# Two residual gates reach all partitions through the tensor engine instead of through DMA

## The chip, the cores and the metric

The kernel runs on one core of one Trainium2 chip. The metric is device microseconds (us) of one execution, lower is better.

## The reference

One layer of a hybrid diffusion backbone, for 512 latent tokens and 256 context tokens of 1024 channels, all in float32. What matters here is the modulation of the latent stream and where its six parts go:

```python
sh1, sc1, gt1, sh2, sc2, gt2 = adaln(c, w_ada, b_ada)         # silu(c) @ w_ada + b_ada, 1024 values each
h = modulate(rms_norm(x, g_mix), sh1, sc1)
mix = concat(fourier_mix(u), rec_mixer(q, v, ...)) @ w_out     # u, q, v, two forget gates, g = split(h @ w_in)
x = x + gt1 * mix
x = x + gt2 * ec_moe(modulate(rms_norm(x, g_ffn), sh2, sc2), ...)   # 16 experts, 64 tokens each
return rms_norm(x, g_final)
```

The gates gt1 and gt2 scale the columns of a product whose rows are tokens, so the kernel wants each of them as one row of 1024 values that stands on every partition.

## The kernel before, in words

**The stages.** Up to about 320 us of the profile the mixer runs (modulation, the input projection in segments of 512 columns, the gated recurrence per head, the Fourier groups), then the output projection and the routing, and from about 370 us the sixteen experts, whose weights (554 MB) stream through a ring of 13 slots of SBUF. The ring's first loads (`load_ahead`, line 1354) wait in SP's queue until the memory of the mixer is free.

**The input projection.** A float32 product is made from high and low parts: ACT casts a loaded half tile to its high part (`split`, line 304), POOL or DVE subtracts it for the low part (line 309), and TensorE runs three matmuls per block (`mm3`, lines 145 to 147). A segment has four steps; the weights of the next step are loaded and split while a step runs. A segment's results stand in four PSUM banks for the latent tokens (`acc`) and, where the context is projected too, in two banks (`c`). The banks `m` and `z` exist once each. In the first step of a segment the units go bank after bank, the two context banks last, with 12 matmuls of 256 columns for each. The segments here are `ff` and `fb` (forward and backward forget gates) and then `v`.

**The modulation's second and third group.** `AdaGroup` 1 holds gt1 and sh2, `AdaGroup` 2 holds sc2 and gt2, 2048 columns each. `step` loads 128 rows of `w_ada` (1 MB, tile `adabuf`, three in turn, line 378 in SP's queue) and DVE adds their products to `adaacc` (lines 383, 385). `finish` adds over the partitions on TensorE (line 398, bank `z`), DVE adds the bias into a row tile `adag` (line 400), and four transposes into bank `m` (line 403, `adagT`) put the values in columns. The row tile has tag `gcc` with two buffers:

```python
brow = pc.tile([P, 512], F32, tag="gcc", bufs=2, name=f"brow{g}")    # 390
row = pc.tile([P, 512], F32, tag="gcc", bufs=2, name=f"adag{g}")     # 395
g = pc.tile([P, 2, CT], F32, tag="gcc", bufs=2, name=f"gcc{d}_{b}")  # 543, in ctx_states
```

so the second tile of the context's states (line 543), which POOL opens with a memset (line 544) and DVE fills (lines 549, 551), takes over the buffer of the row and has to wait until all that reads the row has done so. Its transposes (`kcT`, line 558, bank `m`), ACT's copy of them (line 560) and the products `s0p` (line 566) follow.

**The gates.** The row of gt1 is in `adag` of group 1, on partitions 0 and 32 (512 values each). Two transfers in ACT's queue (line 589) read each of these rows 128 times and write the tile `gt1b` (128 x 1024, 512 KB). gt2 is on partitions 64 and 96 of group 2's row; two transfers (line 615) read them 64 times each into `gt2b` (128 x 512, 256 KB: the first half of the channels on partitions 0 to 63, the second on 64 to 127). `gt1b` is read by `gate_cols` (line 915), first at 235 us, `gt2b` by line 1459, first at 442 us.

**What sets the order.** Each engine executes its instructions in one fixed order, written when the program is built. From line 517 to 666, where the change lies, a list scheduler makes that order from the order of the code and from estimated times; from line 667 on, the order on PE, DVE, ACT and POOL is the one of the code. The sigmoids of lines 526 and 532 (ACT) evict a segment's banks; the second of line 526 frees the last context bank for the next segment.

Of the kernel before, what the change touches and what calls it, by code (L numbers as in the profile page):

```python
# [51 lines left out]
# columns of the packed small operands  # L52
# [8 lines left out]
# and of its matrices  # L61
# [4 lines left out]
# columns of the packed shape constants  # L66
# [16 lines left out]
def hybrid_kernel(ctx: ExitStack, tc, x, ctxt, small, const, pos, w_ada, b_ada, w_in, w_out,  # L83
# [13 lines left out]
    # ------------------------------------------------------------------ memory that stays  # L97
# [25 lines left out]
    # ------------------------------------------------------------------ loads, in the order of use  # L123
# [31 lines left out]
    # ------------------------------------------------------------------ adaLN  # L155
    # silu(c) | silu(c_ctx), padded to one column group
    # forget-gate floor: softmax of the logits over the layers, first row
# [18 lines left out]
    class AdaFirst:  # L176
        """Shift and scale of the mixer for channel blocks 2n and 2n+1."""

        def __init__(self, n):
            self.n = n  # L180
            if n % 2 == 0:
                # the memory of the values and of the context's gates
                w = p1b.tile([P, 2, 4, 256], F32, tag="v", name=f"adaw{n}_v")
                self.w = [w[:, 0], w[:, 1]] + [pc.tile([P, 4, 256], F32, tag=f"fctx{d}", name=f"adaw{n}_{d}")
                                               for d in range(2)]
            else:
                self.w = [wst.tile([P, 4, 256], F32, tag="wh" if t % 2 else "wl", bufs=SB, name=f"adaw{n}_{t}")
                          for t in range(4)]
            for t in range(4):
                # half of the rows of both halves of the sum  # L190
                h, a = divmod(t, 2)
                c0 = a * D + n * 256
                for half in range(2):
                    k0 = 4 * half + 2 * h
                    nc.sync.dma_start(self.w[2 * a + half][:, 2 * h:2 * h + 2],
                                      w_ada[k0 * P:(k0 + 2) * P, c0:c0 + 256].rearrange("(b p) d -> p b d", p=P))

        def part(self, t):
            if t == 0:
                self.acc = bank("m" if self.n == 0 else "z", f"adaA{self.n}")  # L200
            # shifts and scales, each from the first and the last half of the sum: partial sums 2a + b // 2
# [7 lines left out]
        def finish(self):  # L209
# [8 lines left out]
            # row r of the pair, shift or scale, channel block  # L218
# [10 lines left out]
    # ------------------------------------------------------------------ normalise and transpose  # L229
    # the transposed rows wait in the memory of the gates  # L230
# [28 lines left out]
    # high and low parts, channel blocks 4-7 and 0-3  # L259
# [23 lines left out]
    # ------------------------------------------------------------------ input projection  # L283
    class Segment:
        """Columns col..col+512 of the projection, four steps of 256 channels each."""
# [10 lines left out]
        def split(self, kk, a, high=None, low=None):  # L296
            """High and low parts of half a tile."""
# [16 lines left out]
        def units(self, kk):  # L314
            """One step, in units of one 128x128 block of weights against all its tokens."""
# [33 lines left out]
            if kk in self.by_bank:  # L349
                # bank after bank: the last finish, and the next's first are needed, one by one  # L350
# [16 lines left out]
    class AdaGroup:  # L367
        """Columns g*2048..(g+1)*2048 of the modulation of the latent stream."""
# [4 lines left out]
        def step(self, k):  # L373
# [6 lines left out]
            # the products per channel of the sum; the tensor engine adds over the partitions  # L380
# [7 lines left out]
        def finish(self):  # L388
# [15 lines left out]
            return row, raw(tp[:], 0, [[32, 4], [P, 4]])  # L404
# [13 lines left out]
    # columns that add the partial sums  # L418
# [3 lines left out]
    # the first segment follows the modulation by quarters of the channels  # L422
    opening = ExitStack()
    opening.enter_context(tc.manual_schedule(engines={EN.PE, EN.DVE, EN.Activation, EN.Pool, EN.SP}))
    # the clock of the tensor engine rises with its activity, so it is kept active until the rows are there
# [35 lines left out]
    for n in range(4):  # L461
        for k in (2 * n, 2 * n + 1):
            if n == 0:
                # the first weights meanwhile
                modulate(k, 0, lambda: sq.split(0, k, nv.tensor_copy, nv if k == 0 else ng))
            else:
                modulate(k, 0)
# [39 lines left out]
    # the gates, per head: forward, backward, queries  # L507
# [31 lines left out]
    def ctx_states(d):  # L539
        """Final states of the context in one direction, two heads at a time."""  # L540
        gs = []
        for b in range(2):
            g = pc.tile([P, 2, CT], F32, tag="gcc", bufs=2, name=f"gcc{d}_{b}")
            ng.memset(g[:, :, CT - 1:CT] if d == 0 else g[:, :, 0:1], 1.0)
            for a in range(2):
                # running product of the later (earlier) gates
# [3 lines left out]
            # minus the decayed keys  # L550
# [33 lines left out]
    arow1, atp = ag1.finish()  # L584
    sh2 = pz.tile([P, NK], F32, name="sh2")
    nv.tensor_copy(sh2.rearrange("p (j i) -> p j i", j=2), atp[:, 2:4, :])
    for j in range(2):
        src = arow1[32 * j:32 * j + 1, :]
        ns.dma_start(gt1b[:, j * 512:(j + 1) * 512],
                     bass.AP(src.tensor, src.offset, [list(src.ap[0]), [0, P], [1, 512]]))  # L590
# [17 lines left out]
    arow2, atp = ag2.finish()  # L608
    a2 = pz.tile([P, NK], F32, name="a2")
    nv.scalar_tensor_tensor(a2.rearrange("p (j i) -> p j i", j=2), atp[:, 0:2, :], 1.0,  # L610
                            sm[:, C_GFFN:C_GFFN + 8].rearrange("p (j i) -> p j i", j=2),
                            op0=ALU.add, op1=ALU.mult)
    for j in range(2):
        src = arow2[64 + 32 * j:65 + 32 * j, :]
        ns.dma_start(gt2b[64 * j:64 * j + 64, :],
                     bass.AP(src.tensor, src.offset, [list(src.ap[0]), [0, 64], [1, 512]]))
# [6 lines left out]
    class Filler:  # L623
        """Work without close dependences, to be issued between the steps of the heads.

        What waits for a unit's matmuls is issued behind the next unit's.
        """
# [17 lines left out]
        def take(self, n):  # L645
            """Issues units; returns the tensor engine's time, negative where nothing should follow at once."""
# [22 lines left out]
    # the table of the function that the gate needs, loaded ahead  # L669
# [27 lines left out]
    # ------------------------------------------------------------------ HGRN2 heads  # L697
# [8 lines left out]
    def head_init(h):  # L706
        f, q = fq[:, h, 0:2, :], fq[:, h, 2, :]
        # slots: keys forward, queries backward, queries forward, keys backward
# [3 lines left out]
        def merge(B, g):  # L712
            # keys: forward in the first half of a pair of blocks, backward in the second
# [31 lines left out]
    def head_scores(h):  # L745
        """Decayed keys and queries by doubling, with the scores of each level."""
# [71 lines left out]
    def lead(n):  # L818
        # units between a step and what it waits for
# [86 lines left out]
    # ------------------------------------------------------------------ output projection, weights  # L906
# [6 lines left out]
    def gate_cols(k, a, eng):  # L913
        # the residual gate scales the columns
# [19 lines left out]
    # ------------------------------------------------------------------ Fourier groups  # L934
# [3 lines left out]
    def after_u():  # L938
        u_sb = p1b.tile([P, NH, S], F32, tag="u", name="u_sb")

        def wo_step(k, n):
            # the weights of the output projection, a piece at a time
# [30 lines left out]
        def fold(g, eng):  # L973
            # positions m and 512-m folded: even part for the cosines, odd part, in place, for the sines
# [18 lines left out]
        def positions(g):  # L993
# [10 lines left out]
            def evict():  # L1004
                # positions 0 and 256 of the cosines; even frequencies stand first
# [93 lines left out]
    class Steps:  # L1099
        """A generator with the tensor engine's time of each step."""  # L1100
# [19 lines left out]
    def fill_to(t, n=99):  # L1120
        """Issues units until the tensor engine has t us of work, n at most."""
# [41 lines left out]
    # ------------------------------------------------------------------ output projection, residual  # L1163
    px = tc.alloc_tile_pool(name="px", bufs=1, side="left", reuse_waits="tile")
    acc_x = px.tile([P, 4, D], F32, name="acc_x")
    # expert weights: one ring of equal slots
# [12 lines left out]
    # ------------------------------------------------------------------ routing  # L1179
# [20 lines left out]
    # rows of shifts through the router, the same on every partition  # L1200
    sh2r = pq.tile([P, NK, P], F32, tag="x2t", bufs=2, name="sh2r")
    ng.tensor_copy(sh2r, sh2[:, :, None].to_broadcast([P, NK, P]))
    # the largest values so far, then those of a token block
    cand = [pq.tile([NE, (CAP if i in (1, 2) else 0) + P], F32, name=f"cand{i}") for i in range(4)]
    # the largest of the first three blocks and of the last, in order
# [5 lines left out]
    # nothing, above the least, equal to it  # L1211
# [45 lines left out]
    def top(n):  # L1257
        """The CAP largest values of a row of candidates, in order."""
# [13 lines left out]
    # the routing of a token block runs between the products of the next ones  # L1272
# [27 lines left out]
    # the largest of two ordered lists: the larger of each value and its opposite in the other  # L1300
# [4 lines left out]
    # chosen are the tokens above the least of the largest, and the first of those equal to it  # L1305
# [5 lines left out]
    # places: those above in order, then the equal ones; places past CAP are no slot's  # L1311
# [22 lines left out]
    # ------------------------------------------------------------------ experts  # L1334
# [27 lines left out]
    # the memory of the first hidden rows holds a slot's worth before  # L1362
# [18 lines left out]
    for e in range(NE):  # L1381
# [26 lines left out]
        # the hidden rows, and their transpose  # L1408
# [7 lines left out]
        # one-hot rows of the slots with their gates, transposed  # L1416
# [13 lines left out]
        # inner index half*1408 + p*11 + r on partition p  # L1430
# [11 lines left out]
        for s8 in range(8):  # L1442
# [4 lines left out]
            # runs of one row half that lie in this slot  # L1447
# [21 lines left out]
    # the last expert goes down in blocks of columns, so that little is left after its last load  # L1469
# [5 lines left out]
    # the final gain on every partition  # L1475
# [12 lines left out]
    def down_last(n):  # L1488
# [3 lines left out]
        for ih in range(2):  # L1492
# [4 lines left out]
            for r in range(NROW):  # L1497
                # two partial sums, of even and odd rows, that the combination adds
# [7 lines left out]
    def combine_last(n, db):  # L1506
# [6 lines left out]
        for b in range(0, 4, nb):  # L1513
# [12 lines left out]
            # final norm  # L1526
# [31 lines left out]
def _shape_constants():  # L1558
# [6 lines left out]
    # the rows of the sines in the order 256, 255 .. 129 and 128, 127 .. 1  # L1565
# [57 lines left out]
```

## Time and profile before

| | |
|---|---|
| runs | 1670.42, 1672.88, 1674.80 us; median 1672.88 |
| span of the profiled execution, first to last instruction | 1668.7 us |
| busy, share of the span | PE 92%, DVE 24%, ACT 15%, POOL 10% |
| DMA, mean over the span | 363 GB/s from HBM, 424 GB/s in most slices after 375 us |

The profile is of one execution of its own; it gives the span, 4.2 us under the median of the runs, and no other time for it. In the rows below, L followed by a number is a line of the code, `x4` counts instructions that are merged in one row, and a bracket holds the idle time of the engine before the instruction and what ended it. PE is TensorE, SPq and ACTq are the queues in which SP and ACT issue transfers (q1 and q10 in the list of DMA queues). PEclk is TensorE's granted clock, 1.00 being 2.4 GHz.

### The profile page before, as it was taken

To read this page: it belongs to the slowest core of one execution; us is meant where nothing else is said; L and a number is where in the kernel's file an instruction comes from. 1 tells how busy PE (TensorE), PEld (TensorE's weight loads), DVE (VectorE), ACT (ScalarE), POOL (GpSimd) and SP (SyncE) were. 2 spreads that over 40 slices of the span, in tenths; PEclk is the share of its full clock that TensorE was granted. 3 is DMA by queue.
4 is the path that set the end of the run, shared out by engine and by line. 5 is a ranking of instruction groups with operands and counts; after the bars stand their busy time and mean duration, and the time that the engine had idled before them with its cause. 6 is when DMAs were issued, how large, how long until landed. Compare 5 with 4: busy or idle time off the path is not lost.

```text
span 1668.7 us, 19918 instructions
## 1 busy us (share of the span) xinstructions
PE 1529.1 (92%) x8519; PEld 753.1 (45%) x8519; DVE 399.8 (24%) x754; ACT 255.9 (15%) x578; POOL 164.8 (10%) x153
## 2 busy tenths in 40 slices
PE   9978998989999999999898989988988899889897
PEld 6766776874443334343433343334333433243335
DVE  4855678370201010201011001100110111011103
ACT  4512456331000001000100010001000100010002
POOL 2623547400000000000000000000000000000002
PEclk9999999999999989999999998999999989999899
DMA  9785211859999999999999999999999999999998
GB/s 346 283 218 136 77 59 58 334 215 357 422 425 423 424 423 423 423 424 423 424 423 424 424 424 424 423 424 424 423 424 423 423 424 423 424 424 423 424 384 257
DMA packets 91448, 608.37 MB, mean 365 GB/s; under 512 B 8152, under 2 KB 30424, under 8 KB 41184
## 3 DMA queue, kind: packets, MB, share of 16 engines
q1 hardware_dynamic: 90480, 605.21, 88.6%
q10 hardware_dynamic: 880, 1.89, 1.5%
q8 instruction: 67, 1.10, 0.3%
q14 instruction: 21, 0.17, 0.0%
HBM read 604.18 MB, written 2.10 MB: 363 GB/s over the span
## 4 chain that ended last, share of the span: by engine, by line
DMA 48%; PE 41%; DVE 5%; ACT 2%; issue 1%; POOL 1%; SPq 0%; POOLq 0%; DVEq 0%; ACTq 0%
DMA uw<-in_wu_dram 18%; DMA gw<-in_wg_dram 15%; DMA dw<-in_wd_dram 12%; PE dn L1455 9%; PE g L1403 7%; PE u L1403 6%; PE gp L1375 4%; PE cb L1464 3%; DMA fb1r<-in_w_in_dram 1%; DMA adabuf<-in_w_ada_dram 1%; ACT xst L1377 1%; DVE X L795 1%; PE op L146 1%; PE op L145 1%; PE op L147 1%
## 5 line engine op out<-in xcount | busy, mean ns | idle before, releaser
L1455 PE MATMUL dn<-dw,hid 128*64 128x512 f32 (+1 forms) x1440 | 315.9, 562 | 9.0 <-DMA dw<-in_wd_dram 9.0
L1403 PE MATMUL u<-uw,xst 128*64 128x512 f32 (+1 forms) x1464 | 298.1, 559 | 23.4 <-DMA uw<-in_wu_dram 23.3
L1403 PE MATMUL g<-gw,xst 128*64 128x512 f32 (+1 forms) x1440 | 300.3, 569 | 0.0
L1403 PEld LDWEIGHTS u<-uw,xst 128*64 128x64 f32 x1464 | 102.7, 137 | 216.0 <-issue 165.1
L1455 PEld LDWEIGHTS dn<-dw,hid 128*64 128x64 f32 x1440 | 113.9, 136 | 168.1 <-issue 126.5
L1403 PEld LDWEIGHTS g<-gw,xst 128*64 128x64 f32 x1440 | 102.7, 139 | 187.0 <-issue 181.6
L1429 DVE TENSOR_TENSOR hid<-u,hid 128x512 f32<-128x512 f32 (+1 forms) x48 | 30.3, 647 | 538.5 <-PE u L1403 522.6
L1464 PE MATMUL cb<-ye,oht 64*128 64x512 f32 x240 | 108.9, 742 | 26.6 <-DVE acc_x L1467 15.6
L1415 ACT ACTIVATE hid<-g 128x512 f32<-128x512 f32 (+1 forms) x48 | 26.7, 561 | 655.2 <-PE g L1403 654.5
L1473 POOL COPY gt2f<-gt2b 64x512 f32<-64x512 f32 x2 | 1.2, 606 | 1265.8 <-DVE hid L1429 1265.8
L1375 PE MATMUL gp<-oh,xn 128*128 128x128 f32 x512 | 84.0, 294 | 23.3 <-ACT xst L1377 23.1
L1375 PEld LDWEIGHTS gp<-oh,xn 128*128 128x128 f32 x512 | 65.0, 190 | 74.5 <-issue 40.0
L1467 DVE TENSOR_TENSOR acc_x<-cb,acc_x 128x512 f32<-128x512 f32 x120 | 78.6, 688 | 57.6 <-PE cb L1464 57.6
L1377 ACT ACTIVATE xst<-gp,sh,a 128x128 f32<-128x128 f32 x64 | 29.3, 457 | 335.2 <-PE gp L1375 178.9
L1464 PEld LDWEIGHTS cb<-ye,oht 64*128 64x128 f32 x240 | 35.3, 206 | 97.2 <-DVE acc_x L1467 73.0
L1459 DVE TENSOR_TENSOR ye<-dn,gt2b 128x512 f32<-128x512 f32 x15 | 10.4, 692 | 214.9 <-PE dn L1455 214.9
L1437 ACT COPY hid<-hT 128x512 f32<-128x512 f32 (+1 forms) x48 | 24.8, 549 | 170.2 <-PE hT L1435 170.2
L1385 DVE TENSOR_TENSOR oh<-iota,posm 128x512 f32<-128x512 f32 x8 | 5.5, 692 | 182.8 <-PE gp L1375 182.7
L385 DVE SCALAR_TENSOR_TENSOR adaacc<-adabuf,cs,adaacc 128x1024 f32<-128x1024 f32 x28 | 44.3, 1642 | 5.1 <-DMA adabuf<-in_w_ada_dram 5.1
L1419 DVE TENSOR_SCALAR ohg<-iota,posm,aff 128x128 f32<-128x128 f32 x64 | 17.9, 343 | 103.2 <-PE ohT L1424 103.2
L1435 PE MATMUL hT<-ident,hid 128*128 128x128 f32 x176 | 29.3, 300 | 7.7 <-DVE hid L1429 5.9
L1435 PEld LDWEIGHTS hT<-ident,hid 128*128 128x128 f32 x176 | 23.9, 212 | 16.0 <-DVE hid L1429 11.6
(602 smaller groups left out, 1530.6 us busy)
## 6 DMA issues: line engine op xcount, KB each, us to landing
uw<-in_wu_dram SPq DMA_DIRECT2D x122, 1408.0 KB, 27.1
dw<-in_wd_dram SPq DMA_DIRECT2D x120, 1408.0 KB, 27.1
gw<-in_wg_dram SPq DMA_DIRECT2D x120, 1408.0 KB, 27.1
adabuf<-in_w_ada_dram SPq DMA_DIRECT2D x16, 1024.0 KB, 6.4
gw0a<-in_wg_dram SPq DMA_DIRECT2D x7, 1408.0 KB, 15.3
uw0a<-in_wu_dram SPq DMA_DIRECT2D x6, 1408.0 KB, 12.3
adaw<-in_w_ada_dram SPq DMA_DIRECT2D x24, 256.0 KB, 7.6
dw<-in_wd_dram SPq DMA_DIRECT2D x6, 768.0 KB, 13.9
```

Source lines behind the costliest of these rows:

```text
L385: nv.scalar_tensor_tensor(self.acc[:, a], w[:, a], cs[:, k, :1], self.acc[:, a], op0=ALU.mult, op1=ALU.add)
L1375: nt.matmul(gather.gp[:, o:o + P], lhsT=xn[:, i, k * P:(k + 1) * P], rhs=oh[:, i].rearrange("p a j -> p (a j)"), start=(i == 0), stop=(i = ...
L1377: ns.activation(xst[:, k].rearrange("p a j -> p (a j)"), gather.gp[:, o:o + P], AF.Identity, bias=sh2[:, k:k + 1], scale=a2[:, k:k + 1])
L1403: nt.matmul(b[i][64 * hf:64 * hf + 64, :n], lhsT=xst[:, k, e % 2, :], rhs=t[:, hf * HALF + c0:hf * HALF + c0 + n], start=(k == 0), stop=(k ...
L1415: ns.activation(hid[:, c0:c0 + n], gb[i][:, :n], AF.Silu)
L1419: nv.tensor_scalar(ohg[:, i], iota[:, None, :].to_broadcast([P, 2, CAP]), posm[:, i, e:e + 1], aff[:, i, e:e + 1], op0=ALU.is_equal, op1=A ...
L1429: nv.tensor_tensor(hid[:, c0:c0 + n], ub[i][:, :n], hid[:, c0:c0 + n], op=ALU.mult)
L1435: nt.transpose(tp[:, (r - r0) * P:(r - r0 + 1) * P], hid.rearrange("p (f r) -> p r f", r=NROW)[:, r, :], ident)
L1437: ns.copy(hidT[:, r0:r0 + n].rearrange("p r j -> p (r j)"), tp[:, :n * P])
L1455: nt.matmul(db[64 * dh:64 * dh + 64, c0:c0 + n], lhsT=hidT[:, r, 64 * ih:64 * ih + 64], rhs=t[:, o:o + n], start=(ih == 0 and r == 0), sto ...
L1464: nt.matmul(cb, lhsT=oht[hs, i * P:(i + 1) * P], rhs=ye[hs, :], start=True, stop=True, tile_position=(64 * dh, 0))
L1467: nv.tensor_tensor(acc_x[:, i, ds_], cb, acc_x[:, i, ds_], op=ALU.add)
```

## The change

For each gate DVE copies its eight columns (channel block k on column k) from bank `m` to SBUF. A new function `spread` takes four of these columns, broadcasts each along the free dimension to 128 x 128 and transposes it on TensorE into a quarter of bank `m`; the result is the gate's row on every partition. ACT copies the bank to `gt1b` or `gt2b`. The four transfers and the use of the row tile by them are gone; `finish` returns the columns alone. The tiles `gt1c` and `gt2c` are new, 8 values per partition. The rest of the diff removes comments.

```diff
@@ AdaGroup.finish @@
             for i in range(4):
                 nt.transpose(tp[:, i * P:(i + 1) * P], row[:, i * P:(i + 1) * P], ident)
-            return row, raw(tp[:], 0, [[32, 4], [P, 4]])
+            return raw(tp[:], 0, [[32, 4], [P, 4]])
...
     gt1b = hl.tile([P, D], F32, name="gt1b")
-    arow1, atp = ag1.finish()
+
+    def spread(cols, j, name):
+
+        tp = bank("m", name)
+        for i in range(4):
+            nt.transpose(tp[:, i * P:(i + 1) * P], cols[:, 4 * j + i:4 * j + i + 1].to_broadcast([P, P]), ident)
+        return tp
+
+    atp = ag1.finish()
     sh2 = pz.tile([P, NK], F32, name="sh2")
+    gt1c = pc.tile([P, NK], F32, tag="gtc", bufs=2, name="gt1c")
+    nv.tensor_copy(gt1c.rearrange("p (j i) -> p j i", j=2), atp[:, 0:2, :])
     nv.tensor_copy(sh2.rearrange("p (j i) -> p j i", j=2), atp[:, 2:4, :])
     for j in range(2):
-        src = arow1[32 * j:32 * j + 1, :]
-        ns.dma_start(gt1b[:, j * 512:(j + 1) * 512],
-                     bass.AP(src.tensor, src.offset, [list(src.ap[0]), [0, P], [1, 512]]))
+        ns.copy(gt1b[:, j * 512:(j + 1) * 512], spread(gt1c, j, f"gt1s{j}"))
     ag2.step(0)
...
-    arow2, atp = ag2.finish()
+    atp = ag2.finish()
     a2 = pz.tile([P, NK], F32, name="a2")
+    gt2c = pc.tile([P, NK], F32, tag="gtc", bufs=2, name="gt2c")
+    nv.tensor_copy(gt2c.rearrange("p (j i) -> p j i", j=2), atp[:, 2:4, :])
     nv.scalar_tensor_tensor(a2.rearrange("p (j i) -> p j i", j=2), atp[:, 0:2, :], 1.0,
                             sm[:, C_GFFN:C_GFFN + 8].rearrange("p (j i) -> p j i", j=2),
                             op0=ALU.add, op1=ALU.mult)
     for j in range(2):
-        src = arow2[64 + 32 * j:65 + 32 * j, :]
-        ns.dma_start(gt2b[64 * j:64 * j + 64, :],
-                     bass.AP(src.tensor, src.offset, [list(src.ap[0]), [0, 64], [1, 512]]))
+        ns.copy(gt2b[64 * j:64 * j + 64, :], spread(gt2c, j, f"gt2s{j}")[64 * j:64 * j + 64, :])
```

## Rows read from the trace of the kernel before

**Rows 1.** The page, part 4: the chain that ended last, by engine

```profile
DMA 48%; PE 41%; DVE 5%; ACT 2%; issue 1%; POOL 1%; SPq 0%; POOLq 0%; DVEq 0%; ACTq 0%
```

**Rows 2.** Chain of waits, 85 to 260 us: start us, length us, what

```profile
94.39 23.32 DMA fb1r<-in_w_in_dram
...
126.06 0.44 PE kcT L558 x4
...
153.30 10.69 DMA gt2b<-adag
```

**Rows 3.** Windows: stretch, length, busy of five engines (instructions), PEclk, DMA share, GB/s

```profile
90.00:94.00 4.00, 4.00 (x26) 3.41 (x24) 3.45 (x3) 0.00 (x0) 1.17 (x1) 1.00 0.75 252
...
112.00:116.00 4.00, 0.00 (x0) 0.00 (x0) 0.00 (x0) 0.00 (x0) 0.00 (x0) 0.98 0.97 64
```

**Rows 4.** DMA queues, 102 to 106 us: packets, MB, share of 16 engines

```profile
q10 hardware_dynamic: 53, 0.11, 90.9%
q1 hardware_dynamic: 54, 0.11, 7.1%
```

**Rows 5.** PE timeline, 109-124 us: start, length (us), instruction, idle before

```profile
110.50 0.28 PE L146 MATMUL fb_c<-hctx_h,fb0wl 128*128 128x256 f32 x1
110.61 0.28 PE L147 MATMUL fb_c<-hctx_l,fb0wh 128*128 128x256 f32 x1
119.48 0.58 PE L145 MATMUL fb_c<-hctx_h,fb0wh 128*128 128x256 f32 x1 [8.59 <-ACT fctx L526]
...
122.91 0.40 PE L147 MATMUL fb_l<-hlB,fb1wh 128*128 128x512 f32 x1
```

**Rows 6.** Timeline of PE, 148 to 182 us

```profile
150.85 1.07 PE L398 MATMUL ada<-adaacc,ones 128*32 128x512 f32 x8
...
157.97 0.39 PE L146 MATMUL v_l<-v1wh,hlB 128*128 128x512 f32 x1
165.88 0.80 PE L147 MATMUL v_l<-v1wl,hlB 128*128 128x512 f32 x1 [7.53 <-POOL v1wl L309]
...
170.63 0.39 PE L145 MATMUL v_l<-v1wh,hlB 128*128 128x512 f32 x1
...
173.41 0.40 PE L146 MATMUL v_l<-v1wh,hlB 128*128 128x512 f32 x1
173.64 0.39 PE L147 MATMUL v_l<-v1wl,hlB 128*128 128x512 f32 x1
...
174.68 0.48 PE L145 MATMUL v_l<-v1wh,hlB 128*128 128x512 f32 x1
```

**Rows 7.** Timeline of POOL, 80 to 182 us

```profile
164.13 0.10 POOL L544 MEMSET gcc<- 128x2 f32 x1 [11.23 <-DMA gt2b<-adag]
164.24 3.19 POOL L309 TENSOR_TENSOR v1wl<-v1r,v1wh 128x512 fp32r<-128x512 f32 x2
```

**Rows 8.** Timeline of ACT, 80 to 182 us

```profile
117.79 1.14 ACT L304 CAST fb1wh<-fb1r 128x512 fp32r<-128x512 f32 x2 [14.55 <-DMA fb1r<-in_w_in_dram]
...
126.53 0.59 ACT L560 COPY kct<-kcT 128x512 f32<-128x512 f32 x1 [0.95 <-PE kcT L558]
```

**Rows 9.** Timeline of SP's queue, 80 to 182 us

```profile
90.05 4.25 SPq L378 DMA_DIRECT2D adabuf<-in_w_ada_dram  x3
94.39 0.39 SPq L133 DMA_DIRECT2D fb1r<-in_w_in_dram  x1
```

**Rows 10.** Timeline of DVE, 80 to 182 us

```profile
97.05 0.16 DVE L586 COPY sh<-adagT 128x8 f32<-128x8 f32 x1
...
138.67 2.82 DVE L385 SCALAR_TENSOR_TENSOR adaacc<-adabuf,cs,adaacc 128x1024 f32<-128x1024 f32 x2 [1.85 <-DMA adabuf<-in_w_ada_dram]
```

**Rows 11.** Line 1480's instructions: count, min/median/max ns, first and last start

```profile
L1480 PE MATMUL gfT<-ident,gcol x8: 272/273/323, 1589.3 to 1628.4; 128*128 128x128 f32 x8
```

**Rows 12.** Timeline of DVE, 1620 to 1640 us

```profile
1628.66 0.69 DVE L1481 COPY hid<-gfT 128x512 f32<-128x512 f32 x1 [0.90 <-PE gfT L1480]
```

**Rows 13.** Waits of SP's queue, 60 to 400 us: total us, times, longest us

```profile
SPq L1354 <- PE affT L1254: 30.8, 1, 30.8
```
## The prediction, made before the changed kernel was seen

> **What bounds the kernel now.** I read the page first, for what sets the end. Its chain of waits gives DMA 48% and PE 41% [rows 1], nearly all of it in the experts, where weights stream without a gap. The gates are made far ahead of that, near 95 and 153 us, so the change can only move the start of the stream. Whether it does is read from the front's own part of the chain. There two transfers stand out: the load of the weights `fb1r`, 23.3 us from issue to landing, and the broadcast into `gt2b` itself, 10.7 us [rows 2]. The rest of that stretch is a thread of short matmuls and vector steps, so these two are the places to look at.
>
> The windows show the first. From 90 to 94 us the core's DMA engines moved 252 GB/s while TensorE was busy throughout; from 112 to 116 us they were just as occupied (share 0.97), moved 64 GB/s, and TensorE did nothing [rows 3]. The list of queues says with what: between 102 and 106 us, q10 (ACT's, the `gt1b` broadcast) and q1 (SP's, all the loads) moved the same number of packets and bytes, but q10's packets hold 90.9% of the engines' time and q1's 7.1% [rows 4]. The queues take turns packet by packet, and a packet that reads the one row takes some 13 times as long as a load's. So the loads crawl at the broadcast's pace.
>
> The timelines then show who pays. `fb1r` is issued at 94.39 behind three loads of `w_ada` [rows 9]; ACT stands before its cast for 14.55 us [rows 8], and behind that cast in ACT's order stands the sigmoid that frees the last context bank. TensorE waits 8.59 us for exactly that sigmoid and runs its next matmuls at about half speed [rows 5]. At the second place POOL's memset waits 11.23 us for `gt2b`, because the buffer that it opens still holds the row being read; behind it in POOL's order stands the low part `v1wl` [rows 7], and TensorE waits 7.53 us for that [rows 6].
>
> **What goes.** *First stall.* From the matmul at 110.61 to the one at 122.91 TensorE took 12.30 us [rows 5]. Between them lie the 12 matmuls of the last context bank and two of 512 columns. Unstalled, 256 columns come every 0.11 us [rows 5] and 512 every 0.23 us [rows 6]: 13 x 0.11 + 2 x 0.23 = 1.89 us. Loss: 10.4 us. It goes if `fb1r` lands by about 109 us (the cast's 1.14 us and a sigmoid of 0.6 us before 110.7). The three 1 MB loads and `fb1r`, 3.7 MB from 90.05 us on [rows 9], even at the 252 GB/s of the window before the broadcast [rows 3] are through after 14.6 us, at 104.6 us. I take the whole 10.4 us.
>
> *Second stall.* From 157.97 to 170.63 us there are 12.66 us [rows 6]. At full speed the same work is 0.23 us to the next matmul, 1.04 us for it and the `s0p` group (173.64 to 174.68), and six matmuls of 0.23 us [rows 6]: 2.65 us. Loss: 10.0 us. Without the transfer the row's last reader is the four transposes behind it, on TensorE's own path, so the memset needs only those, and POOL's 3.19 us for both halves of `v1wl` [rows 7] start some 10 us earlier. I take all of it. Together 20.4 us.
>
> *What is late next.* Group 2's partial sums: DVE's last ones begin at 138.67 us and take 2.82 us [rows 10], TensorE wants them at 150.85 us [rows 6], 9.4 us later. When TensorE comes 10.4 us earlier this margin is gone, unless DVE comes earlier too; it does, since DVE now stands behind the same sigmoid in the first stall, and its loads are the ones the broadcast slows. I price this at nothing; if only the loads held DVE, it would cost about 1 us.
>
> **What comes.** Sixteen transposes on TensorE in four groups. A group of four, moved through bank `m`, holds TensorE's path for 0.44 us [rows 2], and a transpose of a broadcast column, which the kernel has once, at its end, takes 272 ns from start to end [rows 11], pipelined like any. 4 x 0.44 = 1.8 us, all on the path. By the rows these overlap one another. The Trainium skill, "TensorE: Matmul & The Clock Gate", Part 4: PE-mode transpose, says that a transpose took about 275 ns in one kernel's context, most of it access latency, which is this trace's duration, but not its price: sixteen end to end would be an estimated 4.4 us, and the forecast 2.6 us later.
>
> The waits around them no row shows, since nothing in the front sends two groups through bank `m` with a copy between. The nearest is the final gain, the same four transposes and copy twice: after one copy 0.90 us pass until the next can start [rows 12], and ACT's copy of a bank takes 0.59 us [rows 8]. If TensorE is held for that whole round trip, a group costs 1.49 - 0.44 = 1.05 us more, four of them 4.2 us; if it finds other matmuls in between, nothing; waits that did not exist cannot give a gain. What is queued behind is, on TensorE, the projection, on ACT the sigmoids that free the banks for it. I take 1.0 us, one group of four held, because here, unlike at the end, matmuls of the projection are ready at both places. DVE's two copies of eight columns, 0.16 us each as the one there now [rows 10], stand where `sh2` is copied and are hidden by the projection; uncovered, they would add 0.3 us. ACT's four copies, 4 x 0.59 = 2.4 us [rows 8], take the place of four issues in the same queue, and ACT stands idle around them; uncovered they are in the 4.2 us above. SP's and POOL's queues get nothing new; both lose a wait.
>
> **The sum.** 10.4 + 10.0 - 1.8 - 1.0 = 17.6 us less. The profiled execution spans 1668.7 us and would span 1651.1; the median of the runs, 1672.88, lies 4.2 us above that span, and becomes 1655.3. The shift reaches the end if the stream of expert weights starts earlier by the same, and SP's queue waits for the routing before it loads ahead (30.8 us for the transposed affinities alone) [rows 13].
>
> **The rivals.** *The load is late by itself* (0.10). `fb1r` stands behind 3 MB in its own queue, and the engines were 0.75 occupied before the broadcast came [rows 3]. Then the first stall stays: 1655.3 + 10.4 = 1665.7 us. Against it is the 104.6 us worked out above, more than 4 us early.
>
> *The stream sets the end anyway* (0.07). DMA holds 48% of the chain [rows 1]; if the ring's loads did not start earlier, or had slack, the gain would sink into them: 1672.9 us, no difference. Against it, the first loads wait on the front's results [rows 13].
>
> *Held in bank `m`* (0.05, the other side). The bank exists once, so a gate's second group needs ACT's copy of the first; if the fixed order puts that copy behind a cast that awaits its weights, TensorE stands in its own order until the load lands. Such a cast has waited 14.55 us [rows 8]. Twice that is 29.1 us, with the 1.8 us and against 20.4 us a loss of 10.5: 1683.4 us. It decides from about 9.3 us of hold at each place ((20.4 - 1.8) / 2). For it: a hold needs only one unlucky place in the order. Against it: with the broadcast gone, no load should keep a cast so long.
>
> **How the numbers follow.** The forecast has 0.78. Its own bounds are 20.4 - 1.8 = 18.6 and 18.6 - 4.2 = 14.4 us of gain, 1654.3 to 1658.5 us; with the 2.2 us by which the runs spread around their median, and a little for what is late next, 1651 to 1661. The range must reach the late load too: 1650 to 1668 leaves out the other two rivals and little else. About 0.3%, 5 us, is what a measurement here can tell from no change, so faster means under 1667.9: the forecast and nearly all of the late load, 0.87; same 0.08; slower 0.05.
>
> **What would show it.** In the changed kernel's profile no packets of q10 should be left near 95 to 165 us, the windows from 100 to 116 us should move loads at over 200 GB/s, ACT's cast of `fb1r` should start before 106 us, TensorE's two idle gaps of 8.59 and 7.53 us should be gone and its clock stay at 1.00, and the memset of line 544 should wait for no transfer. The first expert load, the first gather and the end should all come about 17 us earlier. If TensorE shows gaps of over 2 us before the new transposes, bank `m` is the cost that I have too small; if the front is shorter and the end is not, the stream was the bound.

## The result, and the profile of the changed kernel

The changed kernel takes 1653.28 us (median of 4 runs, 1652.53 to 1653.81), the kernel before 1673.07 us beside it: ratio 0.9885, 95% interval 0.9871 to 0.9899, 19.8 us faster. Measured again beside the experiments, the same code took 1653.41 against 1671.70 us (ratio 0.9890, 0.9877 to 0.9903), 18.3 us. The profiled execution spans 1651.7 us and took 1653.81 us, so 2.1 us lie around the span.

The rows of the changed kernel that answer to those of before, first the chain by engine, which answers to [rows 1]:

```profile
PE 50%; DMA 41%; DVE 5%; ACT 2%; issue 1%; SPq 0%; POOL 0%; POOLq 0%; DVEq 0%; ACTq 0%
```

The stream of weights and TensorE still share the end. The two transfers of [rows 2] are no longer among the long pieces of the chain's stretch from 85 to 260 us. The windows, in the columns of [rows 3]:

```profile
100.00:104.00 4.00, 4.00 (x28) 3.63 (x27) 4.00 (x6) 2.66 (x6) 0.67 (x1) 1.00 1.05 422
...
112.00:116.00 4.00, 4.00 (x26) 3.51 (x25) 4.00 (x4) 0.00 (x0) 4.00 (x2) 1.00 0.01 2
```

and the queues between 102 and 106 us, as in [rows 4], where q10 now has no row at all:

```profile
q1 hardware_dynamic: 215, 1.63, 99.9%
```

In the window that moved 64 GB/s with TensorE idle, TensorE is busy throughout at a granted clock of 1.00 and the DMA engines have nothing to move (2 GB/s): the loads issued so far are through, since from 100 to 104 us they ran at 422 GB/s, and SP's queue waits for DVE to free the buffers of the next ones. So the sign of over 200 GB/s up to 116 us came out only until the loads were done. ACT's timeline shows `fb1r` cast without a wait, where it stood for 14.55 us [rows 8], and the new copy into `gt1b` ahead of it:

```profile
98.26 0.59 ACT L598 COPY gt1b<-gt1s 128x512 f32<-128x512 f32 x1 [0.54 <-PE gt1s L589]
...
102.65 1.13 ACT L304 CAST fb1wh<-fb1r 128x512 fp32r<-128x512 f32 x2
```

TensorE's timeline has the new transposes (line 589) between matmuls of the projection and no gap where the first stall was [rows 5]; the last context bank's matmuls run straight into the next step:

```profile
97.39 0.40 PE L147 MATMUL ff_l<-hlA,ff3wh 128*128 128x512 f32 x1
97.62 0.60 PE L589 MATMUL gt1s<-ident,gt1c 128*128 128x128 f32 x4
97.98 0.48 PE L145 MATMUL ff_l<-hlA,ff3wh 128*128 128x512 f32 x1
...
112.89 0.28 PE L147 MATMUL fb_c<-hctx_l,fb0wh 128*128 128x256 f32 x1
113.01 0.39 PE L145 MATMUL fb_l<-hlB,fb1wh 128*128 128x512 f32 x1
```

At the second place the memset of line 544 waits 0.65 us for the four transposes, not 11.23 us for a transfer [rows 7], and `v1wl` follows at once:

```profile
96.68 0.49 POOL L544 MEMSET gcc<- 128x2 f32 x1 [0.17 <-PE adagT L403]
...
144.14 0.10 POOL L544 MEMSET gcc<- 128x2 f32 x1 [0.65 <-PE adagT L403]
144.23 3.14 POOL L309 TENSOR_TENSOR v1wl<-v1r,v1wh 128x512 fp32r<-128x512 f32 x2
```

and TensorE runs from the sums over the partitions through the two new groups to the third step of `v` (its first matmul was at 175.46 us before) without the 7.53 us [rows 6]:

```profile
141.45 1.07 PE L398 MATMUL ada<-adaacc,ones 128*32 128x512 f32 x8
...
144.91 0.62 PE L589 MATMUL gt2s<-ident,gt2c 128*128 128x128 f32 x4
...
146.30 0.60 PE L589 MATMUL gt2s<-ident,gt2c 128*128 128x128 f32 x4
...
157.31 0.39 PE L145 MATMUL v_l<-v2wh,hlA 128*128 128x512 f32 x1
```

DVE's last partial sums now begin at 124.04 us, 14.6 us earlier than in [rows 10], so the 9.4 us ahead of their reader have grown to 13.6 us (141.45 less 127.84 us):

```profile
124.04 3.80 DVE L385 SCALAR_TENSOR_TENSOR adaacc<-adabuf,cs,adaacc 128x1024 f32<-128x1024 f32 x2 [0.65 <-DMA adabuf<-in_w_ada_dram]
```

How the two stalls carry to the end is best read as a table of milestones, each the start of an instruction in the profile of that kernel, in us: the first matmul of `fb`'s second step (after the first stall), of `v`'s third step (after the second), the first ring load in SP's queue, the first gather of the experts, and the span. The other kernels are those of the experiments.

| kernel | `fb` step 2 | `v` step 3 | first ring load | first gather | span |
|---|---|---|---|---|---|
| before | 122.21 | 175.46 | 300.23 | 371.76 | 1668.7 |
| changed | 113.01 | 157.31 | 282.23 | 353.43 | 1651.7 |
| changed, again | 112.89 | 157.12 | 281.99 | 353.42 | 1650.0 |
| gt1 only | 113.08 | 166.01 | 290.48 | 361.93 | 1658.7 |
| gt2 only | 122.21 | 167.42 | 293.52 | 364.68 | 1663.1 |
| own row | 121.70 | 165.43 | 290.39 | 361.82 | 1659.0 |
| own source | 111.90 | 154.92 | 279.37 | 350.89 | 1648.5 |
| 32 rows | 113.21 | 156.55 | 282.71 | 353.88 | 1650.5 |
| thrice | 115.88 | 165.66 | 290.06 | 361.13 | 1658.8 |
| late | 114.53 | 157.87 | 282.29 | 354.36 | 1649.3 |
| late, again | 113.40 | 156.73 | 281.23 | 353.87 | 1648.6 |
| 34 dummies | 113.03 | 157.36 | 282.16 | 353.70 | 1650.6 |
| both late | 111.87 | 155.10 | 282.19 | 353.27 | 1647.9 |

From the first ring load to the end it is 1365.7 to 1369.6 us in all thirteen. The end follows the start of the stream, whatever moved it, within some 2 us.

### The profile page after: what moved, and what is told of

It is laid out like the page before. It is cut to its first block, busy times and chain, and to the rows that moved or that the text cites. A ratio compares the mean times of both kernels' runs of the same rounds, so it can differ in the third digit from the quotient of the medians.

```text
span 1651.7 us, 19945 instructions
## 1 busy us (share of the span) xinstructions
PE 1524.2 (92%) x8535; PEld 750.8 (45%) x8535; DVE 401.5 (24%) x756; ACT 258.0 (16%) x582; POOL 166.7 (10%) x153
## 4 chain that ended last, share of the span: by engine, by line
PE 50%; DMA 41%; DVE 5%; ACT 2%; issue 1%; SPq 0%; POOL 0%; POOLq 0%; DVEq 0%; ACTq 0%
DMA uw<-in_wu_dram 18%; DMA dw<-in_wd_dram 12%; PE dn L1463 10%; DMA gw<-in_wg_dram 10%; PE g L1411 9%; PE u L1411 6%; PE gp L1383 4%; PE cb L1472 4%; ACT xst L1385 1%; DVE X L803 1%; DVE acc_x L1475 1%; PE op L145 1%; PE op L146 1%; PE op L147 1%; PE hT L1443 1%
## 5 line engine op out<-in xcount | busy, mean ns | idle before, releaser
L1467 DVE TENSOR_TENSOR ye<-dn,gt2b 128x512 f32<-128x512 f32 x15 | 10.4, 692 | 211.7 <-PE dn L1463 211.7
```

## The experiments

**One gate at a time.** First gt1 by transposes and gt2 by transfers, then the other way round (in both cuts `finish` gives back the row again for the gate that is transferred):

```diff
...
-    for j in range(2):
-        ns.copy(gt2b[64 * j:64 * j + 64, :], spread(gt2c, j, f"gt2s{j}")[64 * j:64 * j + 64, :])
+    for j in range(2):
+        src = arow2[64 + 32 * j:65 + 32 * j, :]
+        ns.dma_start(gt2b[64 * j:64 * j + 64, :],
+                     bass.AP(src.tensor, src.offset, [list(src.ap[0]), [0, 64], [1, 512]]))
```

> gt1 goes through the tensor engine, gt2 still through the two transfers. Two separate stalls (the theory): the first, 10.4 us, goes, two groups of transposes come (0.9 us); the second, 10.0 us, stays as it was: 1673.1 - 9.5 = 1663.6 us, and in the trace the wait of the memset of line 544 for gt2b of about 11 us. One shared cause (rival: what ends the second stall is set by the first): nearly the whole gain here, 1654 to 1656 us, or nearly none, 1672 us.

1662.70 us against 1672.04 (ratio 0.9945, 0.9930 to 0.9960), 9.3 us less. POOL's memset still waits for gt2b:

```profile
154.82 0.10 POOL L544 MEMSET gcc<- 128x2 f32 x1 [11.34 <-DMA gt2b<-adag]
```

```diff
...
-        ns.copy(gt1b[:, j * 512:(j + 1) * 512], spread(gt1c, j, f"gt1s{j}"))
+        src = arow1[32 * j:32 * j + 1, :]
+        ns.dma_start(gt1b[:, j * 512:(j + 1) * 512],
+                     bass.AP(src.tensor, src.offset, [list(src.ap[0]), [0, P], [1, 512]]))
```

> gt2 goes through the tensor engine, gt1 still through the two transfers. Theory: the first stall stays at 10.4 us with the loads at the broadcast's pace between 100 and 116 us, the second goes: 1673.1 - 10.0 + 0.9 = 1664.0 us. Rival (one shared cause): 1654 to 1656 or 1672 us.

1663.82 us (ratio 0.9953, 0.9938 to 0.9968), 8.2 us less where 9.1 were expected, which the interval (5 to 10 us) does not tell apart. TensorE's first stall is as before:

```profile
119.49 0.58 PE L145 MATMUL fb_c<-hctx_h,fb0wh 128*128 128x256 f32 x1 [8.49 <-ACT fctx L526]
```

The stalls are two, and separate. Their sum by the first gather is 9.83 + 7.08 = 16.9 us against 18.3 us with both. Of the 1.4 us some 0.7 are missing by `v`'s third step (9.45 + 8.04 against 18.15), the rest between there and the first ring load, in the heads, where the kernel with gt2 alone falls from 8.04 to 6.71 us early. That was not followed up.

**A buffer of its own for the row**, all transfers kept, no transposes:

```diff
-            row = pc.tile([P, 512], F32, tag="gcc", bufs=2, name=f"adag{g}")
+            row = pc.tile([P, 512], F32, tag="arow", bufs=1, name=f"adag{g}")
```

> The kernel before, with one edit: the row that the transfers read has a buffer of its own, so no memset waits for them; all four transfers stay. Theory: the first stall is one of traffic (the loads crawl) and stays, the second is one of a buffer and goes: 1673.1 - 10.0 = 1663 us, with no transposes added. Rival A, both are buffer waits: 1652.7 us. Rival B, both are traffic: 1673 us.

1662.26 us (ratio 0.9944, 0.9929 to 0.9959), 9.8 us less, as the theory has it. The first stall stays, and the queues between 102 and 106 us look as in [rows 4]:

```profile
118.97 0.58 PE L145 MATMUL fb_c<-hctx_h,fb0wh 128*128 128x256 f32 x1 [8.29 <-ACT fctx L526]
```

```profile
q10 hardware_dynamic: 58, 0.11, 94.7%
q1 hardware_dynamic: 60, 0.12, 7.9%
```

while the memset, which now opens another buffer, waits only for the sum that makes the row and reads the bias from that buffer, though gt2b's transfer still holds 91.6% of the engines between 158 and 162 us:

```profile
152.69 0.10 POOL L544 MEMSET gcc<- 128x2 f32 x1 [8.21 <-DVE adag L400]
```

So the same kind of transfer costs 10 us in two ways: at the first place by what it does to the other queue, at the second, where no load is wanted, only through the buffer that it holds. At the first place it held its row's buffer too: in the kernel before, POOL's memset waited for it to 117.90 us, as late as `fb1r`'s cast (117.79 us), and the low part `fb1wl` stands behind that memset:

```profile
117.90 0.10 POOL L544 MEMSET gcc<- 128x2 f32 x1 [21.39 <-DMA gt1b<-adag]
```

Taking this hold away alone gave 0.5 us at `fb`'s second step (121.70 against 122.21 us). What quick loads would have given with the hold left in place was not run.

**The same bytes from all partitions.** Each partition's transfer reads that partition's own part of the row tile, which leaves the gates' values out:

```diff
...
-        src = arow1[32 * j:32 * j + 1, :]
-        ns.dma_start(gt1b[:, j * 512:(j + 1) * 512],
-                     bass.AP(src.tensor, src.offset, [list(src.ap[0]), [0, P], [1, 512]]))
+        ns.dma_start(gt1b[:, j * 512:(j + 1) * 512], arow1)
...
+        ns.dma_start(gt2b[64 * j:64 * j + 64, :], arow2[64 * j:64 * j + 64, :])
```

> The kernel before, but each partition's transfer reads that partition's own part of the row tile instead of the one row, so the gates' values are left out: same bytes, same queue, same buffers, same issues, only the source is spread over the partitions. Theory (the packets are slow because all read one partition): gt1b lands in under 4 us, fb1r before 104 us, both stalls go with no transposes: 1673.1 - 20.4 = 1652.7 us. Rival (any transfer of 768 KB from SBUF to SBUF in a second queue does it): no change, 1673 us, or a part of the gain in proportion.

1650.42 us (ratio 0.9875, 0.9858 to 0.9891), 21.6 us less. Queue, bytes and issues are those of before; only the source is spread, and the window and the queues are

```profile
100.00:104.00 4.00, 4.00 (x31) 3.80 (x30) 4.00 (x6) 1.54 (x4) 0.00 (x0) 1.00 1.05 406
```

```profile
q1 hardware_dynamic: 285, 1.45, 88.1%
q10 hardware_dynamic: 132, 0.23, 14.9%
```

406 GB/s where the one row left 79 to 97 in the same window of the three profiles that have it (before, gt2 only, own row), and q10's 132 packets take 14.9% of the engines where 53 took 90.9% [rows 4]. One packet that reads the one row thus held an engine about 15 times as long (90.9 / 53 against 14.9 / 132). The rival, that any such transfer in a second queue does it, is out. One part of the expectation missed: `gt1b` does not land in under 4 us, and the memsets still wait for the transfers, the first for 8.91 us, since these now share the engines with the loads,

```profile
105.22 0.10 POOL L544 MEMSET gcc<- 128x2 f32 x1 [8.91 <-DMA gt1b<-adag]
...
145.15 0.10 POOL L544 MEMSET gcc<- 128x2 f32 x1 [2.85 <-DMA gt2b<-adag]
```

but nothing behind the first one is late (`fb1r` was cast at 103.94 us), and the second comes in time. This kernel has no transposes, so it also gives the two stalls alone: by the first score of the heads it is 20.5 us ahead of the kernel before (178.99 to 158.45 us), by the first gather 20.9.

**A transfer that spreads its source and leaves nothing out.** The sums over the partitions already stand on 32 partitions each, so the bias is loaded on all of them and each transfer copies 32 rows:

```diff
-            ng.memset(brow, 0.0)
...
-                nc.sync.dma_start(brow[32 * j:32 * j + 1, :], b_ada[:, c0:c0 + 512])
+                nc.sync.dma_start(brow[32 * j:32 * j + 32, :],
+                                  b_ada[:, c0:c0 + 512].to_broadcast([32, 512]))
...
+        for a in range(4):
+            ns.dma_start(gt1b[32 * a:32 * a + 32, j * 512:(j + 1) * 512], arow1[32 * j:32 * j + 32, :])
...
+        for a in range(2):
+            ns.dma_start(gt2b[64 * j + 32 * a:64 * j + 32 * a + 32, :], arow2[64 + 32 * j:96 + 32 * j, :])
```

> The kernel before, gates by transfers with nothing left out: the sum over the partitions already stands on 32 partitions for each quarter, so the bias is loaded on all 32 and each transfer copies 32 rows to 32 partitions, eight transfers for gt1 and four for gt2 in place of two and two. Theory (one source partition is what makes packets slow): as with the own source, 1650 to 1652.5 us in the runs of that call, 1 to 3 us under the changed kernel, since no transposes stand on the path. Rival: 32 source partitions are still too few, or eight issues in ACT's queue (about 4.6 us) hold the sigmoids behind them: 1654 to 1662 us, over the changed kernel.

1652.51 us (ratio 0.9887, 0.9874 to 0.9900) against 1653.41 for the changed kernel measured beside it; the runs overlap (1651.64 to 1654.24, and 1652.21 to 1653.64), so no difference can be told. The jam is gone here too (327 GB/s from 100 to 104 us), but from the first to the last of eight issues ACT is held for 7.52 us, more than the 4.6 estimated, and the sigmoids behind them start at 104.12 us instead of 97.12:

```profile
96.56 7.52 ACTq L589 DMA_DIRECT2D gt1b<-adag  x8
104.12 0.60 ACT L532 ACTIVATE fq<-ff_l 128x512 f32<-128x512 f32 x1 [17.33 <-DMA gt1b<-adag]
```

**The price of a group.** Each of the four groups with its copy three times:

```diff
-        ns.copy(gt1b[:, j * 512:(j + 1) * 512], spread(gt1c, j, f"gt1s{j}"))
+        for t in range(3):
+            ns.copy(gt1b[:, j * 512:(j + 1) * 512], spread(gt1c, j, f"gt1s{j}{t}"))
```

and the same for gt2. Its base is the changed kernel, measured beside it:

> The changed kernel once more, on the chip and beside the runs that the next three kernels share, as the base for them: 18 to 20 us under the kernel before.

> The changed kernel with each of the four groups of transposes and its copy done three times: eight more groups. Theory (a group costs its time on the tensor engine): 8 x 0.44 = 3.5 us more than the changed kernel. Rival (a group holds the engine for the round trip through bank m): 8 x 1.49 = 11.9 us more.

1660.52 us against 1653.41, 7.1 us more, between the two. The timeline of TensorE at the second place shows both:

```profile
149.13 0.60 PE L589 MATMUL gt2s<-ident,gt2c 128*128 128x128 f32 x4
...
150.50 0.60 PE L589 MATMUL gt2s<-ident,gt2c 128*128 128x128 f32 x4
151.83 0.65 PE L589 MATMUL gt2s<-ident,gt2c 128*128 128x128 f32 x4 [0.72 <-ACT gt2b L626]
153.15 0.65 PE L589 MATMUL gt2s<-ident,gt2c 128*128 128x128 f32 x4 [0.67 <-ACT gt2b L626]
```

While matmuls of the projection are left to stand in between, a group starts 1.37 us after the one before it and costs only its own time (the matmul behind it starts 0.36 us after its first transpose); when the order has none left, the next group starts 1.33 us after the last and TensorE waits 0.7 us of it for ACT. At `v`'s third step this kernel is 8.5 us behind its base, of which 3.0 are there already at `fb`'s second and 1.0 ahead of all the new groups (the row's own transposes start at 96.89 against 95.91 us). So four extra groups cost 2.0 us at the first place, 0.5 each, and 5.5 at the second, 1.4 each.

**gt2's groups in the routing**, where TensorE only runs dummy transposes that keep it active (`gt2c` gets memory of its own for that):

```diff
...
-    for j in range(2):
-        ns.copy(gt2b[64 * j:64 * j + 64, :], spread(gt2c, j, f"gt2s{j}")[64 * j:64 * j + 64, :])
...
-    active(WARM_R[0])
+    for j in range(2):
+        ns.copy(gt2b[64 * j:64 * j + 64, :], spread(gt2c, j, f"gt2s{j}")[64 * j:64 * j + 64, :])
+    active(WARM_R[0] - 8)
```

> The changed kernel, but gt2's two groups and copies stand in the routing, before the first dummy transposes that only keep the engine active (34 in place of 42), far ahead of gt2b's first reader. Theory (the groups were on the path at 145 us and are hidden here): 0.9 us under the changed kernel, up to 1.5 with the idle time around them. Rival (they were hidden where they are): no difference, or slower by up to 1.5 us if the routing waits for them.

1650.46 us (ratio 0.9875, 0.9862 to 0.9888), 2.95 us under the changed kernel, more than expected. So it was run again, beside the changed kernel with only the fewer dummies:

> The kernel of the run before (gt2's groups in the routing) once more. It was 2.95 us under the changed kernel where the stages of the profiles show some 1.2 us. If the stages tell all, 1651.5 to 1653 us here; if the difference is real in full, 1650 to 1651 us.

> The changed kernel with 34 dummy transposes in the routing in place of 42, and nothing else moved: the second edit of the run with gt2's groups in the routing, alone. If the fewer dummies gave what the stages do not show there, 1651 to 1652 us; if not, as the changed kernel, 1653 to 1654 us.

1651.01 us (1649.98 to 1651.91) again, and 1653.25 us (1652.12 to 1655.27) with 34 dummies alone. The gain of 2 to 3 us over the changed kernel is real, and the fewer dummies alone do not give it. The stages explain some 1.4 us: from `fb`'s second step to the first ring load it is 167.8 us in both late profiles, 169.1 to 169.2 in the three with gt2's groups at their first place. The rest lies after that, in the 1367.0 and 1367.4 us from the first ring load to the end (1368.0 to 1369.5 in those three), and its cause stays open.

**Both gates late**, gt1's groups between the steps of the first head's scores (the late gt2 as above):

```diff
...
         step_all()
+        if n in (3, 5):
+            j = n // 4
+            ns.copy(gt1b[:, j * 512:(j + 1) * 512], spread(gt1c, j, f"gt1s{j}"))
         fill_to(TURN)
```

> Both gates late: gt2's groups in the routing as before, gt1's two groups between the steps of the first head's scores, where the tensor engine has idle gaps of about 1 us. Theory (gt1's groups cost 0.9 to 1.1 us at 97 us and are nearly hidden there): about 1 us under the run with gt2's alone, 1649.5 to 1651 us, the floor being the 1650.4 us with no transposes at all. Rival (the heads' chain has no slack for them): no gain, or 1 us slower.

1650.80 us (1649.97 to 1651.61): inside the range of the theory, but no gain over gt2 alone, so the time does not decide; the stages do. By `v`'s third step it is where the kernel without transposes is (155.10 to 154.92 us), by the first ring load 2.8 us behind it, so the heads' stretch takes back what was won: the rival. Transposes and copies stand in the steps' order there, and ACT's copies start at 171.7 and 181.1 us, 1.9 and 3.8 us after the first of the one group's transposes and the last of the other's, so the bank is held that long:

```profile
L589 PE MATMUL gt1s<-ident,gt1c x8: 272/273/323, 169.8 to 177.3; 128*128 128x128 f32 x8
L1144 ACT COPY gt1b<-gt1s x2: 584/586/587, 171.7 to 181.1; 128x512 f32<-128x512 f32 x2
```

The fastest full kernel of the study is the one with gt2's groups in the routing, 1650.5 and 1651.0 us; both late is level with it.

## Why the prediction was right

Forecast 1655.3 us in a range of 1650 to 1668; measured 1653.3, inside the range and 1.0 us under the forecast's own bounds of 1654.3 to 1658.5. The stalls, the price and the way to the end were the ones named, each by its step:

- *The first stall, 10.4 us.* The own-source kernel starts `fb`'s second step 10.3 us earlier, with nothing else on the path. Of the 10.4 us 8.59 were waiting; most of the rest is the clock, granted at 0.50 from 117 to 120 us in the kernel before, the lower of the two levels, with 0.21 us from matmul to matmul where it was 0.11 ahead of the wait. The bound on when `fb1r` lands (104.6 us) held: ACT casts it at 102.65 us in the changed kernel without a wait. What the prediction did not name is that the broadcast held its row's buffer here as well (21.39 us); the changed kernel takes both away, so the sum did not suffer.
- *The second stall, 10.0 us.* Own row, which takes it away alone, is 10.0 us ahead at `v`'s third step, 0.5 of which it already had at `fb`'s second, so 9.5; own source has 10.2 between the two. Both together, by the first score: 20.5 against the 20.4 of the sum.
- *What is late next* was priced at nothing, and DVE's partial sums have more room than before.
- *What comes, 1.8 + 1.0 us.* Changed against own source is 2.4 us at `v`'s third step and 2.5 at the first gather (353.43 to 350.89): 0.6 us a group, between the 0.44 on the path and the 1.49 of a full round trip, near the 0.70 taken. That a held group costs the round trip is shown by the tripled groups, with 1.3 us from group to group. For the Trainium skill's 275 ns per transpose ("TensorE: Matmul & The Clock Gate", Part 4: PE-mode transpose), end to end, sixteen would have been an estimated 4.4 us; four transposes pushed the next matmul back from 97.62 to 97.98 us, so the trace has them overlapped.
- *The shift reaches the end.* First ring load 18.0 us, first gather 18.3 us earlier, and the stretch from the first ring load to the end the same within 1.0 us (1368.5 and 1369.5). The rival that the stream sets the end anyway is out: it sets the end, but its start moves with the front.
- *The late load* is out by the first item; *held in bank `m`* came to 0.7 us of waiting a group where it was provoked, not to a load's wait: in the changed kernel no cast from 95 to 165 us waits over 5 us for its load.

The difference of 2 us between forecast and median is mostly the base: 17.6 us was forecast, the two milestones moved by 18.0 to 18.3, and the medians differ by 19.8 in the first measurement and 18.3 in the second. The term that was mis-sized is the 4.2 us from span to median: 2.1 us lie around the span, and the profiled execution of before lies low among that kernel's runs (1668.7 us and 2.1 make 1670.8, 2.3 under its median of 1673.07), while that of the changed kernel is the slowest of its four. By the spans 1651.1 us was forecast and 1651.7 came out.

## What to carry to other kernels

A transfer that reads one partition over and over was not paid for in its own time only: the loads of the other queue moved at its pace until it was through (56 to 97 GB/s where the changed kernel has 398 to 422), and its source buffer was held as long. Look for windows in which the DMA engines are busy and the bytes are few, and then ask separately who waits for the bytes and who for the buffer. Here spreading the source over partitions cured it as well as taking the work to TensorE (1652.5 and 1653.4 us), and a buffer of its own cured the second half alone; what the replacement cost depended on whether other work stood between its steps (0.5 or 1.4 us a group), so put it where there is some.

## What the runs showed of the hardware beyond the forecast

- While the one row is read, the two queues move equal numbers of packets (53 to 54, 56 to 54 and 58 to 60 between 102 and 106 us in the three profiles that have it), and the loads get 7.1 to 7.9% of the engines' time: they are held to the slow queue's pace, not to half of the engines. With the source on 128 partitions they moved 1.45 MB in that window in place of 0.11 to 0.12. They had 285 packets to the broadcast's 132 there, in part since the broadcast ends within the window; from 100 to 102 us it was 183 to 155.
- A transpose is 272 ns while the granted clock is 1.00, and 421 ns in the routing of the second late profile, where the window around the moved groups shows 0.50, the lower of the two levels, 1.2 GHz (in the first late profile it shows 0.74, and the transposes take 270 to 473 ns). Work moved into idle time there is longer. The dummies behind it now end so late that the routing's next transpose (`leastT`) starts straight behind them, at 350.96 us in the second late profile, where with 34 dummies alone TensorE waited 1.75 us for DVE before it. The first gather stands 72.1 and 72.6 us behind the first ring load in the late profiles where it was 71.2 to 71.5 in the changed kernel's and that with 34 dummies; the end, which follows the stream, did not feel it:

```profile
L589 PE MATMUL gt2s<-ident,gt2c x8: 417/421/472, 342.4 to 344.8; 128*128 128x128 f32 x8
```

```profile
341.00:346.00 5.00, 3.09 (x14) 2.72 (x15) 4.73 (x28) 3.26 (x7) 0.00 (x0) 0.50 1.01 430
```

- Issuing many small transfers was not free for the issuing engine: an issue took ACT's queue 0.52 to 0.64 us for 64 KB, as for 256 KB at the same place before (0.56 and 0.60). Eight of them are 4.7 us; the rest of the 7.52 us is mostly one stand of 2.4 us between the sixth issue (99.83 us) and the seventh (102.87 us), whose cause no view shows:

```profile
L589 ACTq DMA_DIRECT2D gt1b<-adag x8: 515/602/637, 96.6 to 103.6; - x8
```
